# GpSimd's sums and splits on VectorE, and the first norm's modulation on ScalarE

## Chip, core and metric

One core of a Trainium2 chip runs the kernel once. The metric is the time of the execution on the device in microseconds (us). Five engines work on the core: TensorE (PE in the profile; its weight loads are PEld), VectorE (DVE), ScalarE (ACT), GpSimd (POOL) and SyncE (SP), which issues most of the DMAs. Each has a queue of its own and takes its instructions in order.

## What is computed

One layer of a decoder block in fp32: D = 1024 channels, S = 1024 tokens, a hidden width of 2816. The conditioning vector c gives nine vectors of shift, gain and gate by one product with ada_w. Three branches follow each other, and each begins with an RMS norm and a modulation:

```python
cs = jax.nn.silu(c)
mod = (cs @ ada_w[l] + ada_b[l]).reshape(B, N_MOD, D_MODEL)
sh1, sc1, g1, sh2, sc2, g2, sh3, sc3, g3 = [mod[:, j, None, :] for j in range(N_MOD)]
h = rms_norm(x, norm_ffn1[l]) * (1.0 + sc1) + sh1
x = x + FFN_RESIDUAL * g1 * swiglu(h, ffn1_w_in[l], ffn1_w_out[l])
h = rms_norm(x, norm_mix[l]) * (1.0 + sc2) + sh2
x = x + g2 * token_mixer(h, lb_all[l], mix_w_in[l], ...)
h = rms_norm(x, norm_ffn2[l]) * (1.0 + sc3) + sh3
x = x + FFN_RESIDUAL * g3 * swiglu(h, ffn2_w_in[l], ffn2_w_out[l])
return rms_norm(x, norm_final)
```

rms_norm(x, g) is x / sqrt(mean(x * x) + eps) * g over the channels of a token.

## The kernel before

x lies transposed in SBUF: a tile has 128 channels by 512 tokens. So x is 2 halves of the tokens (h = 0, 1) by 8 tiles of channels (k = 0 to 7), and a norm needs, for each half, a sum of squares over the 8 tiles and then over the partitions.

**Split products.** A product in fp32 is made of three matmuls in fp32r. `split` (L89) makes the two parts of an operand: ScalarE casts the high part (L90), and another engine subtracts it from the source for the low part (L91): VectorE, or GpSimd where `eng` says so. `mmw` (L229) then adds high x high (L232), high x low of the data (L233) and low of the weight x high (L234) in PSUM.

**The three openings.** `paired` (L242) computes the first projections of FFN1, of the token mixer ("mix") and of FFN2. It makes pairs of column blocks by a scheme with 7 products in place of 8, which needs sums of x tiles and of weight tiles. The first two column blocks (`fs`) are computed in the plain way while these sums are still missing; this is the opening: 192 matmuls (2 column blocks, 2 banks, 2 halves, 8 k, 3 parts). `warm_load` loads their weights and splits them, 8 splits of 128x512, the low parts on GpSimd (L268). Behind the opening GpSimd makes 16 subtractions of x tiles (L290), in place; their results are split into `t1` to `t4` by VectorE and ScalarE. `prepare` (L302) loads the weights of one pair of blocks and makes their four sums on VectorE (L306 and L251) and their splits. The loop over the other blocks begins with `prepare` of the first of them.

**The norm.** `squares` (L201) squares the tiles on ScalarE and adds them on VectorE, seven dependent additions (L211). `rows` (L182) sums over the partitions with small matmuls (L188), computes 1/rms of the 512 tokens in `rstd` (L174 to L179) and spreads it: four 128x128 instructions on VectorE (L196) and one matmul (L198) leave r, 128 x 512, in PSUM. `scaled` (L214) multiplies a tile by its column of the gain and by r in one VectorE instruction (L215) and adds the column of the shift on ScalarE (L216).

**FFN1's opening** (`warm` in `run`, L703) has the vectors of its own modulation to compute: for each k two accumulations of 128x1024 on VectorE (`mod`, L154, tiles `ada`), an addition of the bias to each (`mod_bias`, L159), and for the gain one instruction more (`mod_gain`, L163). Then, for each half, `scaled`, the split of the tile (`h` or `bq`), and the matmuls.

A scheduler orders the instructions of each queue by priorities, which follow from the order in which the program is written, and by free buffers: raw weights (tag `raw`) have 3 buffers, split weights (`w`) 11, the parts in `hq` 8 and in `bq` 4.

Of the kernel before, what the change touches and what calls it, by code (L numbers as in the profile page):

```python
# [11 lines left out]
AF = mybir.ActivationFunctionType  # L12
ALU = mybir.AluOpType
# [4 lines left out]
D = 1024  # L18
S = 1024
T = 512  # L20
NK = 8
# [12 lines left out]
C_N1, C_NM, C_N2, C_NF, C_LB, C_HG, C_CB, C_LG, C_LBI = 0, 8, 16, 24, 32, 48, 56, 64, 72  # L34
C_AB = 80
# [5 lines left out]
class Block:  # L41
# [200 lines left out]
    def paired(self, ctx, h, hctx, src, order, warm, emit, after, right, ready=()):  # L242


        nc = self.nc
        V, A = nc.vector, nc.scalar
        sub, add = ALU.subtract, ALU.add
        fs = order[:2]

        def tt(dst, a, b):  # L250
            V.tensor_tensor(dst, a, b, op=sub)  # L251

        def load(f):
            rs = []
            for b in range(2):
                rs.append(self.rp.tile([P, D], F32, tag="raw", name=self.nm("ra")))
                nc.sync.dma_start(rs[b], src(f, b))
            return rs

        self.part(ctx, wp=11, hq=8, bq=4)  # L260
        wop = lambda x: self.parts(x, self.wp, "w")
        hq = lambda x: self.parts(x, self.hq, "hq")


        ws, banks, b1 = {}, {}, dict(ready)

        def warm_load(f):
            ws[f] = [[self.parts(r[:, i * T:(i + 1) * T], self.wp, "w", nc.gpsimd) for i in range(2)] for r in load(f)]  # L268

        def warm_parts(hh, k):  # L270
            if (hh, k) not in b1:
                b1[hh, k] = self.parts(h[1][k], self.bq, "bq") if hh == 1 and k < 4 else self.parts(h[hh][k])

        def warm_mm(f, hh, k):
            if k == 0:
                banks[f, hh] = [self.acc() if f == fs[0] else self.bank() for _ in range(2)]
            for b in range(2):
                self.mmw(banks[f, hh][b], ws[f][b][k // 4], k % 4, b1[hh, k], k == 0, k == NK - 1)

        def warm_end(hh):  # L280
            for f in fs:
                emit(f, hh, *banks[f, hh], None)

        warm(fs, warm_load, warm_parts, warm_mm, warm_end)
        b11, b21, b22 = ([b1[hh, k0 + i] for i in range(4)] for hh, k0 in ((0, 0), (0, 4), (1, 4)))
        t1, t2, t3, t4 = [], [], [], []
        for i in range(4):
            x11, x12, x21, x22 = h[0][i], h[1][i], h[0][4 + i], h[1][4 + i]
            for o, x, y in ((x11, x12, x11), (x12, x22, x12), (x22, x22, x11), (x21, x21, x22)):
                nc.gpsimd.tensor_tensor(o, x, y, op=sub)  # L290
            t2.append(hq(x22))
            t3.append(hq(x12))
            t1.append(self.parts(x11))
            t4.append(self.parts(x21, self.bq, "bq"))
        hctx.close()
        self.part(ctx, right=True, **right)

        def product(ps, w, xs):
            for i in range(4):
                self.mmw(ps, w, i, xs[i], i == 0, i == 3)  # L300

        def prepare(f):  # L302
            ra, rb = load(f)
            a11, a12, a21, a22 = ra[:, :T], ra[:, T:], rb[:, :T], rb[:, T:]
            w11, w12, w22 = wop(a11), wop(a12), wop(a22)
            V.tensor_tensor(a22, a21, a22, op=add)  # L306
            tt(a21, a11, a21)
            tt(a11, a22, a11)
            tt(a12, a12, a11)
            ws2, ws3, ws1, ws4 = wop(a11), wop(a21), wop(a22), wop(a12)  # L310
            return w11, w12, w22, ws1, ws2, ws3, ws4

        ops = None
        for n, f in enumerate(order):
            if f not in fs:
                w11, w12, w22, ws1, ws2, ws3, ws4 = ops if ops else prepare(f)
                ops = prepare(order[n + 1]) if n + 1 < len(order) else None
                p1, p2, p3, p4, p5, p6, p7 = [self.acc() if (7 * n + i) % 2 == 0 else self.bank() for i in range(7)]
                product(p1, w11, b11)
                c11, c21, c22, u = (self.piece() for _ in range(4))  # L320
                A.copy(u, p1)
                product(p2, w12, b21)
                V.tensor_tensor(c11, p2, u, op=add)
                product(p3, ws2, t2)
                V.tensor_tensor(u, p3, u, op=add)
                product(p4, ws3, t3)
                V.tensor_tensor(c22, p4, u, op=add)
                product(p5, w22, t4)
                V.tensor_tensor(c21, p5, c22, op=add)
                emit(f, 0, c11, c21, c21)  # L330
                product(p6, ws1, t1)
                V.tensor_tensor(c22, p6, c22, op=add)
                V.tensor_tensor(u, p6, u, op=add)
                product(p7, ws4, b22)
                V.tensor_tensor(u, p7, u, op=add)  # L335
                emit(f, 1, u, c22, c22)
            after(n, f)
        return b1
# [338 lines left out]
    def run(self):  # L677
        nc, tc, a = self.nc, self.tc, self.a
# [16 lines left out]
        with outer:  # L695
# [7 lines left out]
            def warm(fs, load, parts, mm, end):  # L703
                ada = {}

                def mod_in(k):
                    ada[k] = [self.mod_load(j, k, p, t) for j, p, t in ((1, self.hp, "h"), (0, self.hq, "hq"))]

                def x_in(h):
                    for i in range(4):  # L710
                        nc.sync.dma_start(xt[h][i], a["x"][h, i])

                x_in(0)
                load(fs[0])
                mod_in(0)
                x_in(1)
                mod_in(1)
                mod_in(2)
                r = [self.rows(self.squares(xs[h]), D) for h in range(2)]
                for k in range(NK):  # L720
                    if k + 3 < NK:
                        mod_in(k + 3)
                    if k == 1:
                        load(fs[1])
                    for j in (1, 0):
                        self.mod(j, k, ada[k][1 - j])
                        self.mod_bias(j, k, k + 1)
                    self.mod_gain(1, C_N1, k, k + 1)
                    for h in range(2):
                        self.scaled(xs[h][k], k, r[h], m[1], m[0])  # L730
                        parts(h, k)
                        mm(fs[0], h, k)
                        if k == 2:
                            mm(fs[1], h, 0)
                            mm(fs[1], h, 1)
                        if k >= 2:
                            mm(fs[1], h, k)
                for h in range(2):
                    end(h)
# [282 lines left out]
```

## Time and profile before

| | before |
|---|---|
| median of 3 runs | 2467.28 us (2462.15 to 2468.1) |
| the profiled execution | 2467.12 us |
| its span, first to last instruction | 2465.3 us |
| TensorE busy | 2405.5 us, 98% |
| VectorE busy | 2010.2 us, 82% |
| ScalarE busy | 944.8 us, 38% |
| GpSimd busy | 116.9 us, 5% |

Busy time counts how long an engine had an instruction in work; matmuls overlap in their pipeline, so that one shows 0.39 us where the next starts 0.23 us later. The granted clock (PEclk) is the share of full speed that TensorE was given: 1.00 is 2.4 GHz, and its other level is 1.2 GHz. A time in brackets at the end of a row is the engine's idle time ahead of it, with what ended it.

### The profile page before, as it was taken

How to read it: one execution, taken by the hardware profiler on the slowest of the kernel's cores; microseconds unless marked ns; L12 is line 12 of the kernel's file. 1: busy time of each engine (PE TensorE's matmuls, PEld its weight loads, DVE VectorE, ACT ScalarE, POOL GpSimd, SP SyncE). 2: the span in 40 equal slices, each digit the busy share in tenths (PEclk: the TensorE clock that was granted, in tenths of full speed). 3: DMA queues.
4: the chain of work that ended last, by engine and by line, in shares of the span. 5: the costliest groups of instructions: out<-in, count | busy, mean ns of one | idle time of the engine just before them, and what ended most of it. 6: DMA issues, size and time to landing. Idle time of an engine off the chain costs nothing.

```text
span 2465.3 us, 30875 instructions
## 1 busy us (share of the span) xinstructions
PE 2405.5 (98%) x11320; PEld 1992.7 (81%) x11320; DVE 2010.2 (82%) x3010; ACT 944.8 (38%) x1679; POOL 116.9 (5%) x77
## 2 busy tenths in 40 slices
PE   4999999999999999999999999999999999999997
PEld 3788887888878888788888888888888888888886
DVE  8999999778889999799999877575568777775977
ACT  4522223344644333233333335453343333324443
POOL 3300000000050000000000000000050000000000
PEclk9999999999999999999999999999999999999998
DMA  7156665595523323311212112774523233228743
GB/s 277 68 190 208 202 203 186 174 344 176 171 86 116 106 83 104 105 52 65 68 44 65 56 56 90 241 251 162 159 80 124 86 107 117 93 86 298 269 128 124
DMA packets 139975, 346.46 MB, mean 141 GB/s; under 512 B 15536, under 2 KB 15664, under 8 KB 139824
## 3 DMA queue, kind: packets, MB, share of 16 engines
q1 hardware_dynamic: 139680, 343.97, 41.7%
q8 instruction: 89, 1.46, 0.2%
q10 hardware_dynamic: 144, 0.52, 0.1%
q14 instruction: 62, 0.51, 0.1%
HBM read 266.31 MB, written 78.12 MB: 140 GB/s over the span
## 4 chain that ended last, share of the span: by engine, by line
PE 80%; DVE 12%; DMA 5%; issue 2%; ACT 1%; POOL 0%; SPq 0%; DVEq 0%; ACTq 0%
PE pa L233 8%; PE pa L234 8%; PE pa L232 8%; PE pb L232 8%; PE pb L234 8%; PE pb L233 8%; PE pa L106 8%; PE pa L104 8%; PE pa L105 8%; PE pb L579 3%; DMA ada<-in_ada_w_dram 2%; DVE w L91 2%; DMA ra<-in_ffn_w_in_dram 1%; DVE ada L154 1%; DVE ra L251 1%
## 5 line engine op out<-in xcount | busy, mean ns | idle before, releaser
L90 ACT CAST w<-ra 128x512 fp32r<-128x512 f32 x402 | 238.4, 619 | 436.5 <-DMA ra<-in_ffn_w_in_dram 110.8
L104 PE MATMUL pa<-h,wh 128*128 128x512 f32 x896 | 355.4, 397 | 1.5 <-ACT wh L90 1.5
L106 PE MATMUL pa<-h,wl 128*128 128x512 f32 x896 | 353.7, 395 | 1.8 <-DVE wl L91 1.8
L105 PE MATMUL pa<-h,wh 128*128 128x512 f32 x896 | 353.3, 394 | 0.0
L543 DVE SCALAR_TENSOR_TENSOR uc<-u,par,uc 128x1023 f32<-128x1023 f32 (+14 forms) x240 | 303.1, 1263 | 2.7
L91 DVE TENSOR_TENSOR w<-ra,w 128x512 fp32r<-128x512 f32 x378 | 254.8, 690 | 10.0 <-ACT w L90 9.4
L232 PE MATMUL pa<-h,w 128*128 128x512 f32 x504 | 199.3, 398 | 5.8 <-ACT h L90 4.1
L233 PE MATMUL pa<-h,w 128*128 128x512 f32 x504 | 199.7, 396 | 2.9 <-DVE h L91 2.9
L234 PE MATMUL pb<-h,w 128*128 128x512 f32 x504 | 197.4, 392 | 4.1 <-POOL w L91 4.0
L234 PE MATMUL pa<-h,w 128*128 128x512 f32 x504 | 198.1, 393 | 0.0
L106 PEld LDWEIGHTS pa<-h,wl 128*128 128x128 f32 x896 | 168.6, 188 | 36.0 <-DVE wl L91 2.5
L104 PEld LDWEIGHTS pa<-h,wh 128*128 128x128 f32 x896 | 168.8, 188 | 35.3 <-ACT wh L90 2.3
L233 PE MATMUL pb<-h,w 128*128 128x512 f32 x504 | 197.0, 391 | 0.0
L232 PE MATMUL pb<-h,w 128*128 128x512 f32 x504 | 196.7, 391 | 0.0
L105 PEld LDWEIGHTS pa<-h,wh 128*128 128x128 f32 x896 | 168.9, 189 | 33.2 <-issue 0.7
L90 ACT CAST ob<-br 128x512 fp32r<-128x512 f32 x154 | 95.8, 622 | 198.6 <-PE pb L234 80.1
L90 ACT CAST wh<-raw 128x1024 fp32r<-128x1024 f32 x80 | 84.0, 1051 | 205.5 <-PE pa L105 192.6
L91 DVE TENSOR_TENSOR ob<-br,ob 128x512 fp32r<-128x512 f32 x154 | 106.7, 694 | 67.5 <-ACT ob L90 66.8
L233 PE MATMUL pa<-ob,oa 128*128 128x512 f32 x352 | 137.5, 391 | 1.5 <-DVE ob L91 1.5
L232 PE MATMUL pa<-ob,oa 128*128 128x512 f32 x352 | 137.1, 390 | 0.0
L234 PE MATMUL pa<-ob,oa 128*128 128x512 f32 x352 | 137.0, 389 | 0.0
L360 ACT ACTIVATE s<-c 128x512 f32<-128x512 f32 x80 | 50.6, 633 | 185.4 <-DVE c L335 127.6
(233 smaller groups left out, 5015.6 us busy)
## 6 DMA issues: line engine op xcount, KB each, us to landing
ra<-in_ffn_w_in_dram SPq DMA_DIRECT2D x88, 512.0 KB, 4.2
br<-bd SPq DMA_DIRECT2D x154, 256.0 KB, 3.2
bd<-c SPq DMA_DIRECT2D x146, 256.0 KB, 2.0
ada<-in_ada_w_dram SPq DMA_DIRECT2D x72, 512.0 KB, 4.4
ar<-in_ffn_w_out_dram SPq DMA_DIRECT2D x88, 256.0 KB, 4.5
ra<-in_mix_w_in_dram SPq DMA_DIRECT2D x32, 512.0 KB, 3.8
raw<-in_mix_w_in_dram SPq DMA_DIRECT2D x32, 512.0 KB, 3.5
ar<-in_ffn_w_out_dram SPq DMA_DIRECT2D x22, 512.0 KB, 4.8
```

What stands on the lines that cost most here:

```text
L90: self.nc.scalar.copy(hi, src)
L91: (eng or self.nc.vector).tensor_tensor(lo, src, hi.bitcast(F32), op=ALU.subtract)
L104: mm(ps, wh, x[:, 0, :], start=first, stop=False)
L105: mm(ps, wh, x[:, 1, :], start=False, stop=False)
L106: mm(ps, wl, x[:, 0, :], start=False, stop=last)
L154: self.nc.vector.scalar_tensor_tensor(raw, raw, 1.0, self.cs, op0=ALU.mult, op1=ALU.mult, accum_out=dst)
L232: mm(ps, wh, x[:, 0, :], start=first, stop=False)
L233: mm(ps, wh, x[:, 1, :], start=False, stop=False)
L234: mm(ps, wl, x[:, 0, :], start=False, stop=last)
L360: A.activation(s, a, AF.Silu)
L543: V.scalar_tensor_tensor(uc[:, j:], u[:, :S - j], cw(KC - 1 - j), uc[:, j:], op0=ALU.mult, op1=ALU.add)
L579: mm(ps[0:n, i * 64:(i + 1) * 64], ch(k, i)[:, 0:n], two(ch(qa, i))[:, :, 1, :], start=True, stop=True)
```

## The change

Three edits, in `paired` and in FFN1's opening.

- In `warm_load` the low parts of the first weights are made by VectorE, not GpSimd: 8 splits in each of the three openings.
- The 16 subtractions of x tiles go from GpSimd to VectorE, in the order of four loops and not of one, and `prepare` of the first pair of blocks is written ahead of them. GpSimd is left with a few memsets.
- In FFN1's opening each tile of a half is multiplied by r as soon as r of this half is there (L733 in the new file), all eight tiles ahead of the loop over k. In the loop ScalarE computes the gain and the shift of 128x1 from the accumulations (L742, L743), and applies both to a tile in one instruction (L746). The bias of the gain is prepared once for all k (L728). `mod_bias`, `mod_gain` and `scaled` are no longer used here.

```diff
         def warm_load(f):
-            ws[f] = [[self.parts(r[:, i * T:(i + 1) * T], self.wp, "w", nc.gpsimd) for i in range(2)] for r in load(f)]
+            ws[f] = [[self.parts(r[:, i * T:(i + 1) * T], self.wp, "w") for i in range(2)] for r in load(f)]
...
-        t1, t2, t3, t4 = [], [], [], []
-        for i in range(4):
-            x11, x12, x21, x22 = h[0][i], h[1][i], h[0][4 + i], h[1][4 + i]
-            for o, x, y in ((x11, x12, x11), (x12, x22, x12), (x22, x22, x11), (x21, x21, x22)):
-                nc.gpsimd.tensor_tensor(o, x, y, op=sub)
-            t2.append(hq(x22))
-            t3.append(hq(x12))
-            t1.append(self.parts(x11))
-            t4.append(self.parts(x21, self.bq, "bq"))
-        hctx.close()
...
-        ops = None
+        ops = prepare(order[2])
+
+
+        t1, t2, t3, t4 = [], [], [], []
+        xx = [(h[0][i], h[1][i], h[0][4 + i], h[1][4 + i]) for i in range(4)]
+        for x11, x12, x21, x22 in xx:
+            tt(x11, x12, x11)
+        for x11, x12, x21, x22 in xx:
+            tt(x12, x22, x12)
+            tt(x22, x22, x11)
+            t2.append(hq(x22))
+            t3.append(hq(x12))
+        for x11, x12, x21, x22 in xx:
+            tt(x21, x21, x22)
+            t4.append(self.parts(x21, self.bq, "bq"))
+        for x11, x12, x21, x22 in xx:
+            t1.append(self.parts(x11))
+        hctx.close()
...
-                w11, w12, w22, ws1, ws2, ws3, ws4 = ops if ops else prepare(f)
+                w11, w12, w22, ws1, ws2, ws3, ws4 = ops
...
-                r = [self.rows(self.squares(xs[h]), D) for h in range(2)]
+
+                bg = self.small(NK)
+                V.scalar_tensor_tensor(bg, self.par[:, C_AB + NK:C_AB + 2 * NK], 1.0, self.par[:, C_N1:C_N1 + NK],
+                                       op0=ALU.add, op1=ALU.mult)
+                for h in range(2):
+                    r = self.rows(self.squares(xs[h]), D)
+                    for x in xs[h]:
+                        V.tensor_tensor(x, x, r, op=ALU.mult)
...
+                    gain, shift = m[1][:, k:k + 1], m[0][:, k:k + 1]
                     for j in (1, 0):
                         self.mod(j, k, ada[k][1 - j])
-                        self.mod_bias(j, k, k + 1)
-                    self.mod_gain(1, C_N1, k, k + 1)
+                    A.activation(gain, gain, AF.Identity, bias=bg[:, k:k + 1], scale=self.col(C_N1, k))
+                    A.activation(shift, shift, AF.Identity, bias=self.col(C_AB, k))
                     for h in range(2):
-                        self.scaled(xs[h][k], k, r[h], m[1], m[0])
+                        x = xs[h][k]
+                        A.activation(x, x, AF.Identity, bias=shift, scale=gain)
```

How the queue of VectorE changes is shown at three places. The first is FFN1's opening, from the spread of r of half 1 on (`pb_450` before, `pb_460` now). Tiles `x_311` to `x_314` hold half 0 (two k each), `x_315` to `x_318` half 1; `h_514` and `bq_476` are parts of k = 1 of half 0 and of k = 0 of half 1. Before:

```order
L196 TENSOR_SCALAR s_445<-par,t_437 128x128 x4
L159 TENSOR_TENSOR mod_88<-mod_88,par 128x1
L154 SCALAR_TENSOR_TENSOR ada_362,mod_87<-ada_362,cs 128x1024
L215 SCALAR_TENSOR_TENSOR x_315<-x_315,mod_88,pb_450 128x512
L91 TENSOR_TENSOR h_514<-x_311,h_514 128x512
L215 SCALAR_TENSOR_TENSOR x_315<-x_315,mod_88,pb_450 128x512
L159 TENSOR_TENSOR mod_87<-mod_87,par 128x1
L163 SCALAR_TENSOR_TENSOR mod_88<-mod_88,par 128x1
L91 TENSOR_TENSOR bq_476<-x_315,bq_476 128x512
```

Now, where `w_510` to `w_519` are splits of the second column block's weights and `bq_491` is the part of k = 0 of half 1:

```order
L154 SCALAR_TENSOR_TENSOR ada_470,mod_87<-ada_470,cs 128x1024
L179 SCALAR_TENSOR_TENSOR t_447<-t_448,t_447 128x4
L91 TENSOR_TENSOR w_510<-ra_506,w_510 128x512
L196 TENSOR_SCALAR s_455<-par,t_447 128x128 x4
L91 TENSOR_TENSOR w_513<-ra_506,w_513 128x512
L91 TENSOR_TENSOR w_516<-ra_508,w_516 128x512
L733 TENSOR_TENSOR x_315<-x_315,pb_460 128x512 x2
L733 TENSOR_TENSOR x_316<-x_316,pb_460 128x512 x2
L733 TENSOR_TENSOR x_317<-x_317,pb_460 128x512 x2
L733 TENSOR_TENSOR x_318<-x_318,pb_460 128x512 x2
L91 TENSOR_TENSOR bq_491<-x_315,bq_491 128x512
```

All eight multiplications of the half and three weight splits now stand ahead of its first split. The second place is the mix opening, ahead of the last additions for r of its half 1 (L211). L444 is L451 in the new file (the residual of FFN1); `w_6380` and `w_6300` begin the weights of the first pair. Before:

```order
L444 SCALAR_TENSOR_TENSOR x_4014<-pa_5677,mod_89,x_4014 128x512
L211 TENSOR_TENSOR s_5994<-s_5994,s_6005 128x512
L444 SCALAR_TENSOR_TENSOR x_4014<-pa_5678,mod_89,x_4014 128x512
L444 SCALAR_TENSOR_TENSOR x_4015<-pa_5679,mod_89,x_4015 128x512
L211 TENSOR_TENSOR s_5994<-s_5994,s_6008 128x512
L91 TENSOR_TENSOR w_6380<-ra_6376,w_6380 128x512
L211 TENSOR_TENSOR s_5994<-s_5994,s_6011 128x512
L444 SCALAR_TENSOR_TENSOR x_4015<-pa_5680,mod_89,x_4015 128x512
L91 TENSOR_TENSOR w_6383<-ra_6376,w_6383 128x512
L91 TENSOR_TENSOR w_6386<-ra_6378,w_6386 128x512
L211 TENSOR_TENSOR s_5994<-s_5994,s_6014 128x512
```

Now, from the third L451 on (two more pairs of such splits, `w_5956` to `w_5965`, stand between the first three):

```order
L451 SCALAR_TENSOR_TENSOR x_4009<-pa_5673,mod_89,x_4009 128x512
L91 TENSOR_TENSOR w_5978<-ra_5970,w_5978 128x512
L91 TENSOR_TENSOR w_5981<-ra_5970,w_5981 128x512
L451 SCALAR_TENSOR_TENSOR x_4009<-pa_5674,mod_89,x_4009 128x512
L211 TENSOR_TENSOR s_5988<-s_5988,s_5999 128x512
L91 TENSOR_TENSOR w_6300<-ra_6296,w_6300 128x512
L211 TENSOR_TENSOR s_5988<-s_5988,s_6002 128x512
L91 TENSOR_TENSOR w_6303<-ra_6296,w_6303 128x512
L211 TENSOR_TENSOR s_5988<-s_5988,s_6005 128x512
L91 TENSOR_TENSOR w_6306<-ra_6298,w_6306 128x512
L211 TENSOR_TENSOR s_5988<-s_5988,s_6008 128x512
```

The eight weight splits have come between the four L451, and the last four additions stand behind all of these. The third place is FFN2's opening, around the last addition for r of its half 1. L948 is L964 in the new file (the residual of the token mixer). Before:

```order
L948 SCALAR_TENSOR_TENSOR x_12730<-pa_14367,mod_92,x_12730 128x512
L211 TENSOR_TENSOR s_14500<-s_14500,s_14517 128x512
L948 SCALAR_TENSOR_TENSOR x_12730<-pa_14399,mod_92,x_12730 128x512
L211 TENSOR_TENSOR s_14500<-s_14500,s_14520 128x512
L174 TENSOR_SCALAR t_14528<-pb_14523 128x4
```

Now:

```order
L964 SCALAR_TENSOR_TENSOR x_12724<-pa_14361,mod_92,x_12724 128x512
L91 TENSOR_TENSOR w_14442<-ra_14438,w_14442 128x512
L91 TENSOR_TENSOR w_14445<-ra_14438,w_14445 128x512
L91 TENSOR_TENSOR w_14448<-ra_14440,w_14448 128x512
L91 TENSOR_TENSOR w_14451<-ra_14440,w_14451 128x512
L91 TENSOR_TENSOR w_14458<-ra_14454,w_14458 128x512
L91 TENSOR_TENSOR w_14461<-ra_14454,w_14461 128x512
L211 TENSOR_TENSOR s_14494<-s_14494,s_14514 128x512
L174 TENSOR_SCALAR t_14522<-pb_14517 128x4
```

Six weight splits have come between the last residual and the last addition.

## Rows read from the trace of the kernel before

**Rows 1.** The page: busy time, share of the span and instructions of each engine.

```profile
PE 2405.5 (98%) x11320; PEld 1992.7 (81%) x11320; DVE 2010.2 (82%) x3010; ACT 944.8 (38%) x1679; POOL 116.9 (5%) x77
```

**Rows 2.** Busy time by stretch: length, PE, PEld, DVE, ACT, POOL, granted clock, DMA.

```profile
32.00:98.00 66.00, 55.75 (x194) 40.72 (x195) 65.04 (x104) 34.03 (x58) 35.43 (x20) 0.92 0.20 75
98.00:680.00 582.00, 579.65 (x2548) 476.71 (x2547) 503.50 (x833) 216.46 (x381) 0.00 (x0) 1.00 0.61 204
680.00:720.00 40.00, 36.01 (x146) 28.88 (x145) 29.00 (x48) 19.21 (x33) 15.21 (x11) 0.91 0.30 98
720.00:1000.00 280.00, 280.00 (x1237) 231.91 (x1237) 259.63 (x340) 102.61 (x176) 23.87 (x15) 1.00 0.29 99
1800.00:1860.00 60.00, 60.00 (x268) 49.32 (x267) 46.72 (x60) 31.44 (x57) 36.23 (x24) 1.00 0.19 66
```

**Rows 3.** Waits of TensorE, 32 to 98 us: total, times, longest.

```profile
PE pa L232 <- ACT h L90: 4.1, 3, 2.4
PE pb L234 <- POOL w L91: 4.0, 1, 4.0
PE pa L233 <- DVE h L91: 2.9, 5, 0.9
```

**Rows 4.** Timeline of GpSimd in FFN1's opening: start, length, instruction.

```profile
44.55 3.67 POOL L91 TENSOR_TENSOR w<-ra,w 128x512 fp32r<-128x512 f32 x2 [1.52 <-ACT w L90]
```

**Rows 5.** GpSimd's groups by line: busy, mean ns, idle before.

```profile
L290 POOL TENSOR_TENSOR x<-x,x 128x512 f32<-128x512 f32 x48 | 79.8, 1683 | 55.2 <-ACT x L216 37.9 <-issue 6.6 <-DVE h L91 3.9
L91 POOL TENSOR_TENSOR w<-ra,w 128x512 fp32r<-128x512 f32 x24 | 36.1, 1533 | 1423.6 <-ACT w L90 1423.6
```

**Rows 6.** Timeline of VectorE in FFN1's opening.

```profile
34.15 1.22 DVE L154 SCALAR_TENSOR_TENSOR ada<-ada,cs 128x1024 f32<-128x1024 f32 x1
...
38.34 0.75 DVE L215 SCALAR_TENSOR_TENSOR x<-x,mod,pb 128x512 f32<-128x512 f32 x1 [0.96 <-PE pb L198]
...
41.21 0.68 DVE L91 TENSOR_TENSOR bq<-x,bq 128x512 fp32r<-128x512 f32 x1
...
45.31 1.77 DVE L91 TENSOR_TENSOR h<-x,h 128x512 fp32r<-128x512 f32 x1
47.00 1.24 DVE L159 TENSOR_TENSOR mod<-mod,par 128x1 f32<-128x1 f32 x1
...
56.92 0.68 DVE L91 TENSOR_TENSOR h<-x,h 128x512 fp32r<-128x512 f32 x1
```

**Rows 7.** Timeline of TensorE in FFN1's opening and at its end.

```profile
52.82 0.79 PE L234 MATMUL pb<-h,w 128*128 128x512 f32 x1 [4.02 <-POOL w L91]
...
70.59 0.73 PE L232 MATMUL pa<-h,w 128*128 128x512 f32 x2 [2.40 <-ACT h L90]
...
98.01 0.39 PE L232 MATMUL pa<-h,w 128*128 128x512 f32 x1
```

**Rows 8.** Timeline of ScalarE, a shift of the first norm.

```profile
26.26 0.72 ACT L216 ACTIVATE x<-x,mod 128x512 f32<-128x512 f32 x1 [3.71 <-DVE x L215]
```

**Rows 9.** Timeline of TensorE at the mix opening.

```profile
689.83 0.50 PE L233 MATMUL pa<-ob,oa 128*128 128x512 f32 x1 [1.05 <-DVE ob L91]
...
703.05 1.87 PE L188 MATMUL pb<-ones,s 128*128 128x1 f32 x8 [2.95 <-DVE s L211]
```

**Rows 10.** Timeline of VectorE ahead of the mix opening and in it.

```profile
673.07 4.29 DVE L91 TENSOR_TENSOR h<-x,h 128x512 fp32r<-128x512 f32 x7
...
711.82 5.36 DVE L215 SCALAR_TENSOR_TENSOR x<-x,mod,pb 128x512 f32<-128x512 f32 x8 [3.48 <-PE pb L198]
...
720.74 5.87 DVE L91 TENSOR_TENSOR bq<-x,bq 128x512 fp32r<-128x512 f32 x4 [1.04 <-ACT bq L90]
```

**Rows 11.** Timeline of VectorE in FFN2's opening.

```profile
1811.66 0.69 DVE L211 TENSOR_TENSOR s<-s,s 128x512 f32<-128x512 f32 x1 [0.76 <-ACT s L210]
...
1818.13 5.36 DVE L215 SCALAR_TENSOR_TENSOR x<-x,mod,pb 128x512 f32<-128x512 f32 x8 [1.22 <-PE pb L198]
...
1827.69 4.69 DVE L91 TENSOR_TENSOR bq<-x,bq 128x512 fp32r<-128x512 f32 x4
```

More of the change, by code (lines that the diff above doesn't have):

```diff
@@ L285, in paired @@
         b11, b21, b22 = ([b1[hh, k0 + i] for i in range(4)] for hh, k0 in ((0, 0), (0, 4), (1, 4)))
-        t1, t2, t3, t4 = [], [], [], []
-        for i in range(4):
-            x11, x12, x21, x22 = h[0][i], h[1][i], h[0][4 + i], h[1][4 + i]
-            for o, x, y in ((x11, x12, x11), (x12, x22, x12), (x22, x22, x11), (x21, x21, x22)):
-                nc.gpsimd.tensor_tensor(o, x, y, op=sub)
-            t2.append(hq(x22))
-            t3.append(hq(x12))
-            t1.append(self.parts(x11))
-            t4.append(self.parts(x21, self.bq, "bq"))
-        hctx.close()
[L296 to L300, printed above, removed]
         def prepare(f):
@@ L311, in prepare, with product @@
             return w11, w12, w22, ws1, ws2, ws3, ws4
-        ops = None
+        ops = prepare(order[2])
[14 more added lines that the diff above has]
+        hctx.close()
+        self.part(ctx, right=True, **right)
+        def product(ps, w, xs):
+            for i in range(4):
+                self.mmw(ps, w, i, xs[i], i == 0, i == 3)
         for n, f in enumerate(order):
             if f not in fs:
-                w11, w12, w22, ws1, ws2, ws3, ws4 = ops if ops else prepare(f)
+                w11, w12, w22, ws1, ws2, ws3, ws4 = ops
                 ops = prepare(order[n + 1]) if n + 1 < len(order) else None
```

## The prediction

> **What bounds the kernel now.** I read the busy times first. TensorE is busy 2405.5 of 2465.3 us [rows 1], so only its idle time and its slow stretches can be won back. The table by stretches shows where they are: from 98 to 680 us TensorE is busy 579.65 of 582.00 us, and from 720 to 1000 us all of the time; what the change can reach of the rest lies in 32 to 98 us and, a little, in 680 to 720 us [rows 2]. GpSimd works in just these places: 35.43 us in 32 to 98, 15.21 in 680 to 720, 36.23 in 1800 to 1860, where TensorE is full nevertheless [rows 2].
>
> In 32 to 98 us TensorE runs 194 matmuls [rows 2]. At the steady pitch, 280.00 / 1237 = 0.226 us each [rows 2], they need 43.9 us; 22.1 us are lost. Named waits are 4.1 us for ScalarE's and 2.9 for VectorE's halves of the data, and one of 4.0 us for a weight split on GpSimd [rows 3]; the rest is the lower level of the clock: the granted clock of the stretch is 0.92 [rows 2], a mixture of 1.2 and 2.4 GHz. VectorE is busy 65.04 of the 66.00 us [rows 2]: the data pieces come late because VectorE is full. So VectorE is the bound of this opening, and the steady stretch begins at 98.01 us, at the first of the seven products [rows 7].
>
> VectorE is full partly because its own instructions are long there. A split takes 0.68 us at 56.92, and 1.77 us at 45.31 [rows 6], while two splits of GpSimd's run from 44.55 to 48.22 [rows 4]; a 128x1 addition took 1.24 us at 47.00 [rows 6]. The lines with an operand in PSUM are spared: L215 takes 0.75 us at 38.34 [rows 6] and 0.67 each at 711.82 [rows 10], and no more where it falls inside a piece of GpSimd's.
>
> **The change, part by part.** All sums are made against the profiled execution, 2467.12 us, of which the span is 2465.3; the median of the three is 2467.28, so the one stands for the other.
>
> *GpSimd's work on VectorE.* Each of the three openings (FFN1, mix, FFN2) gives up 8 splits (1.53 us each on GpSimd) and 16 subtractions (1.68 each) [rows 5]. On VectorE an undisturbed 128x512 split or subtraction fills 0.61 us (4.29 for seven in a row) [rows 10]: 24 x 0.61 = 14.6 us more per opening. Against it goes the lengthening. In 32 to 98 us I count about 10 us on splits (up to 1.1 each) and 7 us on the tiny additions, some 17 in all, of which the pairs in rows 6 are samples; the bound from above is all of GpSimd's 35.43 us [rows 2], from below nothing. So VectorE's total hardly moves; what moves is when TensorE is served.
>
> *The first norm.* The 24 small instructions L159 and L163 go; their cost is in the 7 us above. L215 becomes L733 at the same price, 0.67 us with the PSUM operand [rows 10]. ScalarE gets two 128x1 instructions per k and its 16 modulations take a second column operand; no row shows that form, the nearest is L216 with one, 0.72 us [rows 8]. ScalarE is busy 34.03 of 66.00 us [rows 2], so neither is on the path, apart from one in the chain of the first piece. The Trainium skill ("ScalarE: Activation LUTs", What ACT_TABLE_LOAD costs) states about 93 ns for each pointer operand of 128x1, which no run here shows: by it the estimate is 1.5 us on ScalarE, and the sum would be at most 0.3 us higher.
>
> More weighs the order. Of each half all eight multiplications now stand together ahead of its first piece, and all wait for r of that half. I walk VectorE's queue: the first r comes at about 24.6 (it was read at 25.5: four weight splits of 0.6 are put in front of the last addition, the tiny instructions out of it). Four additions are finished by then or shortly after, at 25.5; eight multiplications to 30.9; first piece split at 32.1. The last addition of half 1 ends at 34.5, its row sums are ready 2.2 later at 36.7 (1.87 us of L188 at the lower clock [rows 9] and its way), and five ada accumulations (1.15 us pitch, a row of 1.22) [rows 6], two splits and the tiny instructions stand between there and the spread, which ends at 42.7. The broadcast waits 1.22 us at 1818.13 [rows 11] at full clock; I take 2.2 at the lower one, which gives r of half 1 at 44.9, against 38.34 before [rows 6]. Eight multiplications, 5.3 us, and a split: the first piece of half 1 is whole at 50.8, against 41.9 [rows 6]. Queued behind these multiplications are three weight splits and the splits of all further pieces, and TensorE waits for them.
>
> From there on VectorE needs, per k, two ada accumulations and two splits, 2.3 + 1.2 = 3.5 us; TensorE needs 24 x 0.226 = 5.4. TensorE becomes the bound. By the order 32 of the 192 opening matmuls stand ahead of that piece, 160 behind it: 160 x 0.226 = 36.2 us, so the opening ends at 87.0 at full clock; I add 1 us for a start at the lower level, as behind the waits at 52.82 and 70.59 [rows 7]: 88. The 16 sums, 4 weight sums and the splits that feed the products then stand on VectorE from about 71 to 96; by the same walk the third piece of the second sums is whole at 91 and wanted at 95.5. So **FFN1: 88 against 98, -10 us**, from -12 (no slow stretch, r 1 us earlier) to -6 (two more waits with the slow stretch behind them, 2 us each). The stretch up to 680 is full, so it passes on the whole gain.
>
> *Mix opening.* Before, a split lengthened under GpSimd made TensorE wait 1.05 us at 689.83, and the row sums L188 came 2.95 us late, at 703.05, and took 1.87 us [rows 9], since the clock had gone to its lower level (0.91 in the mean of the stretch [rows 2]). Now VectorE has the eight weight splits between the four L451, which it can hold (1.2 us in a spacing of 2.0), then four additions and three splits, 7 x 0.6 to 0.7, ending near 700.9; 24 matmuls stand ahead of L188 where 15 did, 5.4 us from about 695.3, so TensorE reaches it at 700.8. The wait is nearly gone and with it the slow stretch: 1.2 + 2.9 + about 2: **-6 us**, from -7.5 to -3 (the last addition waits for the third split's data). VectorE's 16 sums lie later, where TensorE was busy 280.00 of 280.00 us beside a VectorE at 259.63 [rows 2], and four splits there take 5.87 us at 720.74 [rows 10] where 2.4 would do.
>
> *FFN2 opening.* Here GpSimd was beside a full TensorE [rows 2], so there is nothing to win. VectorE now has six weight splits between the last L964 (0.75 us from about 1810.2) and the last addition, which began at 1811.66 [rows 11]: the first split is whole at 1811.5, and the third matmul, wanted at 1810.4, waits 1.1 us; the last addition ends at 1815.1, when TensorE has come to L188 as well. Four more splits stand around the spread, so L215 starts at about 1820.7 against 1818.13; the pieces of half 1, split from 1827.69 on [rows 11], still come before TensorE has finished half 0 at about 1835. **+1.4 us**, from 0 to +4 (a slow stretch behind the wait).
>
> Sum: -10 - 6 + 1.4 = -14.6; 2467.12 - 14.6 = 2452.5 us. The ends together are -19.5 and -5; not all fall to one side, so the forecast's own range is 2447 to 2459.
>
> **Rivals.**
> 1. *Half of FFN1's gain goes again.* r of half 1 comes 6.6 us later; if TensorE idles around it more than I give it, stays at the lower level through the first matmuls and stops once more at the weights of the second column, FFN1 gains 4 to 5 us. For it: the two starts in rows 7 each cost more than the wait itself. Against: behind 50.8 VectorE is ahead. Time: 2467.1 - 4.5 - 6 + 1.4 = 2458, 2456 to 2462.
> 2. *VectorE stays the bound.* In its queue four evaluations of the opening's results (L368), which wait for TensorE and ScalarE, stand ahead of the second half of the sums. If they hold the sums up by more than the 4.5 us of margin, the products start 4 us late, and FFN2 shows its +4: 2467.1 - 6 - 6 + 4 = 2459, 2456 to 2463.
> 3. *Slower.* The lengthening isn't GpSimd's doing but comes from DMA or from VectorE itself, and stays. Then 14.6 us per opening are added to a VectorE that is full at 65.04 of 66.00: FFN1 +12, mix +4, FFN2 +2 gives 2485. It decides against me if L91 in 40 to 80 us still has 1.7 us. Against it: the lengthened one at 45.31 lies inside GpSimd's own splits, the short one at 56.92 does not [rows 4, 6], and the PSUM form was spared. The Trainium skill ("SBUF — State Buffer", SBUF: two separate sides) says that a VectorE instruction with two SBUF inputs and a GpSimd instruction that reads SBUF lock each other out for the whole instruction; the trace agrees with the direction, at 1.77 against 0.68 us.
>
> **How the numbers follow.** The forecast has 0.64, rival 1 0.18, rival 2 0.12, rival 3 0.06. What a measurement can tell from no change is about 0.3%, 7.4 us: faster is below 2459.9, slower above 2474.7. The forecast lies wholly below; of rivals 1 and 2 some two fifths lie above. Faster 0.82, same 0.12, slower 0.06. The range leaves out rival 3 and the ends of the others: 2446 to 2461.
>
> **What would show it.** Right: L91 and the small additions in 32 to 98 us at 0.6 to 0.7 us throughout; first piece of half 1 near 51 us and no named wait of TensorE above 1 us behind it; first product at 86 to 90; L188 of the mix opening at 0.95 us without a wait; about 1 us of wait at the third matmul of FFN2. Wrong: a granted clock under 0.95 in 60 to 88 us (rival 1), TensorE waiting for sums behind 88 (rival 2), or splits of 1.7 us without GpSimd (rival 3).

## The result: 21 us faster, outside the range

The changed kernel takes 2444.38 us (median of 4 runs, 2443.83 to 2445.03) against 2465.51 before (2462.15 to 2468.1): a ratio of 0.9915, 95% interval 0.9898 to 0.9932. The direction was forecast, the size was not: 2452.5 was predicted, with 2446 to 2461 as the range.

The page of the changed kernel has GpSimd idle and VectorE no fuller than before, as [rows 1] has it for the kernel before:

```profile
PE 2395.2 (98%) x11320; PEld 1987.2 (81%) x11320; DVE 2000.2 (82%) x3059; ACT 953.2 (39%) x1695; POOL 1.2 (0%) x5
```

The stretches of [rows 2], in the changed kernel (length, PE, PEld, DVE, ACT, POOL, granted clock, DMA):

```profile
32.00:98.00 66.00, 63.01 (x254) 49.42 (x253) 64.00 (x115) 43.81 (x81) 0.00 (x0) 1.00 0.28 103
98.00:680.00 582.00, 581.78 (x2566) 480.43 (x2565) 508.42 (x844) 221.94 (x389) 0.00 (x0) 1.00 0.60 203
680.00:720.00 40.00, 39.40 (x176) 32.00 (x175) 37.27 (x68) 25.22 (x45) 0.00 (x0) 1.00 0.33 119
```

In 32 to 98 us TensorE runs 254 matmuls where 194 ran. The granted clock in that row, 1.00 (0.92 before), says nothing of the row's first 12 us: in both kernels a matmul there still takes 0.63 us, as it does before behind the wait at 52.82 [rows 7], and 0.39 us only from about 45 us on. In the changed kernel:

```profile
40.34 0.63 PE L234 MATMUL pa<-h,w 128*128 128x512 f32 x1
...
45.14 0.39 PE L233 MATMUL pb<-h,w 128*128 128x512 f32 x1
```

From there on the changed kernel stays at full clock, where the kernel before fell back twice (0.54 granted from 54 to 58 us, 0.66 from 70 to 74). In 98 to 680 us, a stretch that I had called full, it runs 18 matmuls more.

Where the time went is read best from a few marks that both programs pass in TensorE's timeline: the first matmul of FFN1's third product (its operand is the first `hq`), the first matmul of the mix opening, the third product of mix, the first matmul of FFN2, the last L188. "Before again" is a second profile of the unchanged kernel, run e5 below.

| stretch, us | before | before again | changed | change (against each profile) | forecast |
|---|---|---|---|---|---|
| start to FFN1's third product | 103.45 | 104.05 | 91.27 | -12.2, -12.8 | -10 |
| to the mix opening | 593.09 | 590.72 | 587.85 | -5.2, -2.9 | -1.2 (put down to the mix opening) |
| to mix's third product | 57.06 | 56.68 | 51.66 | -5.4, -5.0 | -4.8 |
| to FFN2's first matmul | 1056.35 | 1056.19 | 1056.29 | -0.1, +0.1 | 0 |
| to the last L188 | 640.69 | 641.13 | 642.30 | +1.6, +1.2 | +1.4 |
| to the end | 14.66 | 13.93 | 13.83 | -0.8, -0.1 | 0 |
| span | 2465.3 | 2462.7 | 2443.2 | -22.1, -19.5 | -14.6 |

A second profile of the changed kernel (e10) has 91.22, 586.88, 51.40, 1059.14, 642.05 and 14.53 us in these stretches. One of them is 2.9 us longer than in the first profile of the same kernel. So a difference of this size in a single pair of profiles proves little; below, a stretch counts where several profiles agree.

In FFN1's opening TensorE's waits were 11.0 us in [rows 3]; in the changed kernel, 32 to 98 us, all of them lie ahead of 49 us:

```profile
PE pa L233 <- DVE h L91: 2.9, 2, 2.7
PE pa L232 <- ACT h L90: 1.8, 1, 1.8
PE pb L232 <- DVE x L733: 0.6, 1, 0.6
PE pb L188 <- DVE s L211: 0.3, 1, 0.3
```

VectorE's instructions are short, as the groups by line of the changed kernel say (busy, mean ns, idle before):

```profile
L91 DVE TENSOR_TENSOR h<-x,h 128x512 fp32r<-128x512 f32 x48 | 30.6, 684 | 0.0
...
L91 DVE TENSOR_TENSOR hq<-x,hq 128x512 fp32r<-128x512 f32 x24 | 15.4, 686 | 0.0
```

The same two groups of the kernel before:

```profile
L91 DVE TENSOR_TENSOR h<-x,h 128x512 fp32r<-128x512 f32 x48 | 48.1, 1034 | 0.0
...
L91 DVE TENSOR_TENSOR hq<-x,hq 128x512 fp32r<-128x512 f32 x24 | 26.9, 1157 | 0.0
```

That is 29 us less for these 72 splits alone; it pays most of the 44 us that the 72 instructions taken over from GpSimd cost on VectorE, at 0.61 us each.

### The profile page after: what moved, and what is told of

The parts are those of the page before. It is cut to its first block, busy times and chain, and to the rows that moved or that the text cites. A ratio compares the mean times of both kernels' runs of the same rounds, so it can differ in the third digit from the quotient of the medians.

```text
span 2443.2 us, 30741 instructions
## 1 busy us (share of the span) xinstructions
PE 2395.2 (98%) x11320; PEld 1987.2 (81%) x11320; DVE 2000.2 (82%) x3059; ACT 953.2 (39%) x1695; POOL 1.2 (0%) x5
## 4 chain that ended last, share of the span: by engine, by line
PE 95%; DVE 3%; DMA 1%; ACT 1%; issue 0%; SPq 0%; DVEq 0%; ACTq 0%
PE pa L233 11%; PE pa L234 11%; PE pa L232 11%; PE pb L234 10%; PE pb L233 10%; PE pb L232 10%; PE pa L106 8%; PE pa L105 8%; PE pa L104 8%; PE pb L586 4%; PE pb L610 1%; PE pb L625 1%; PE pb L645 1%; PE pb L570 1%; PE pb L647 1%; DVE s L211 0%
## 5 line engine op out<-in xcount | busy, mean ns | idle before, releaser
L91 DVE TENSOR_TENSOR w<-ra,w 128x512 fp32r<-128x512 f32 x402 | 266.7, 687 | 14.5 <-ACT w L90 13.7
```

The lines of the kernel that those rows point to most:

```text
L91: (eng or self.nc.vector).tensor_tensor(lo, src, hi.bitcast(F32), op=ALU.subtract)
```

## The experiments

Each run was compared with the kernel before on the same chip; medians of before were 2464.4 to 2465.7. The three edits of the change were first made one by one.

### e1: the new norm alone

```diff
-                r = [self.rows(self.squares(xs[h]), D) for h in range(2)]
+                for h in range(2):
+                    r = self.rows(self.squares(xs[h]), D)
+                    for x in xs[h]:
+                        V.tensor_tensor(x, x, r, op=ALU.mult)
...
-                        self.scaled(xs[h][k], k, r[h], m[1], m[0])
+                        A.activation(x, x, AF.Identity, bias=shift, scale=gain)
```

> The kernel before with the new first norm alone; GpSimd keeps its splits and sums. Theory A (GpSimd's lengthening of VectorE is what makes FFN1's opening long): splits of up to 1.7 us stay, the first of the seven products still begins at about 96 us against 98.0, total 2464 to 2467 against 2466. Rival B (the gain of the opening is the norm's: fewer small instructions in VectorE's queue): first product near 88 us, total about 2456.

It took 2468.81 us, ratio 1.0019 (1.0010 to 1.0028): 4 us slower than before, and neither theory's time. Its trace shows both a gain and a larger loss. TensorE, 60 to 100 us, in two stretches:

```profile
60.00:80.00 20.00, 20.00 (x90) 16.57 (x89) 20.00 (x21) 13.77 (x27) 13.69 (x8) 1.00 0.00 0
80.00:100.00 20.00, 10.29 (x45) 7.93 (x43) 19.86 (x25) 6.39 (x12) 6.72 (x5) 0.82 0.00 0
```

From 47.6 us on the opening's matmuls run without a gap beside a working GpSimd, and they are done at 90.1 us, 8 us sooner than before. Then TensorE stops, and the first product begins at 101.78:

```profile
101.78 0.80 PE L232 MATMUL pa<-h,w 128*128 128x512 f32 x1 [11.49 <-ACT s L360]
```

ScalarE's timeline there names the chain:

```profile
88.81 0.62 ACT L90 CAST bq<-x 128x512 fp32r<-128x512 f32 x1
98.16 1.66 ACT L90 CAST w<-ra 128x512 fp32r<-128x512 f32 x3 [8.73 <-DVE ra L251]
99.84 1.28 ACT L360 ACT_TABLE_LOAD   x1
101.13 0.60 ACT L360 ACTIVATE s<-pa 128x512 f32<-128x512 f32 x1
```

The product needs the PSUM bank of an opening result. Its evaluation (L360) stands in ScalarE's queue behind the casts of the first pair's weights, which wait 8.73 us for their sums (L251) on VectorE. There splits still take up to 1.78 us beside GpSimd (1.06 us in the mean of all 48 splits of `h`). So the opening can end early without GpSimd's release; what follows it cannot begin.

### e2: GpSimd's work on VectorE alone

```diff
-            ws[f] = [[self.parts(r[:, i * T:(i + 1) * T], self.wp, "w", nc.gpsimd) for i in range(2)] for r in load(f)]
+            ws[f] = [[self.parts(r[:, i * T:(i + 1) * T], self.wp, "w") for i in range(2)] for r in load(f)]
...
-                nc.gpsimd.tensor_tensor(o, x, y, op=sub)
+                tt(o, x, y)
```

> The kernel before with the splits and sums on VectorE, in the old order of the sums, weights of the first pair prepared behind them, old norm. Theory A: first product at about 88 us, mix opening 5 to 6 us shorter, FFN2's about 2 us longer, the stall of 4 us between 340 and 400 us stays, total about 2454. Rival B: first product at 94 or later, total about 2460. Rival C (the stall at 340 to 400 us goes because VectorE is less loaded): no stall, about 2450.

2453.12 us, ratio 0.9955 (0.9940 to 0.9970), near theory A's 2454. But the parts differ: the opening is done at 86.5 us, sooner than A said, and the products behind it wait, as TensorE's timeline shows:

```profile
91.57 0.50 PE L234 MATMUL pa<-h,w 128*128 128x512 f32 x1 [3.98 <-DVE w L91]
...
100.05 0.49 PE L232 MATMUL pa<-hq,w 128*128 128x512 f32 x1 [2.03 <-ACT w L90]
```

A split of the first pair's weights comes too late. And the stretch to the mix opening is 587.1 us, without the loss of before, as rival C had it.

### e3 and e4: the early preparation, added to before and taken from the changed kernel

e3 is the kernel before with this edit alone (the function `prepare` moves up with its call); e4 is the changed kernel with the edit undone.

```diff
+        ops = prepare(order[2])
         t1, t2, t3, t4 = [], [], [], []
...
-        ops = None
...
-                w11, w12, w22, ws1, ws2, ws3, ws4 = ops if ops else prepare(f)
+                w11, w12, w22, ws1, ws2, ws3, ws4 = ops
```

> The kernel before with one edit: the weights of the first pair are prepared ahead of the sums, as in the changed kernel; GpSimd and norm as before. Theory D (the stall of 4 us between 340 and 400 us is the weight loads running out of lead, and the early preparation gives the lead): stall gone, total about 2462. Rival E (the stall is chance in the one profiled execution of before): total within 1 us of before's median, and other executions of before without it.

> The changed kernel with one edit: the weights of the first pair are prepared behind the sums, when the loop over the pairs begins. Theory D: the lead is lost, TensorE waits 4 us or more between 86 and 400 us, total about 2449 against 2444.4. Rival E: no stall, total 2444 to 2445.

e3 took 2462.2 us, ratio 0.9988 (0.9978 to 0.9998); e4 2449.76, ratio 0.9942 (0.9927 to 0.9957). e4's total is what theory D said, but not for D's reason. Its stretch to the mix opening is 587.3 us, with no stall; the whole 6.7 us lie at the start of the products, 97.95 against 91.27, in one wait and in the slow matmuls of 0.63 us that follow it up to 96.2:

```profile
90.49 0.79 PE L234 MATMUL pa<-h,w 128*128 128x512 f32 x1 [3.70 <-DVE w L91]
```

So the early preparation doesn't buy lead for later; it buys the first product's weights. In e3, where TensorE comes to the products only at 99.6, they would have been there anyway, and the total falls by 2 us, of which the stretch behind (588.8 us) has more than all. That is theory D's total, but e1 (588.3) and e2 (587.1) lack the stall too, and they prepare late.

### e5: the kernel before once more

> The kernel before once more, unchanged, for a second profile of it. From the first of the seven products' third (first hq operand) to the start of the mix opening the first profile of before took 593.1 us, and the four kernels run since took 587.1 to 588.8. Rival E (chance of one execution): this profile takes 587 to 589 there and its total is about 2461 to 2463. Theory D': the stall belongs to the order of before and shows again at 592 to 594 us.

2464.46 us, with 590.7 us to the mix opening: between the two ranges. The stall is there again, at the same place and with the same name; TensorE in the second profile:

```profile
389.10 0.50 PE L232 MATMUL pa<-h,w 128*128 128x512 f32 x1 [1.34 <-ACT c L321]
```

and the copy that it waits for, in ScalarE's timeline of the first profile:

```profile
387.95 1.66 ACT L90 CAST w<-ra 128x512 fp32r<-128x512 f32 x3 [1.97 <-DVE ra L251]
389.52 0.58 ACT L321 COPY c<-pa 128x512 f32<-128x512 f32 x1
```

The copy of the first product out of PSUM stands behind three casts that wait for weight sums. So the place belongs to the kernel, and the size varies from one execution to the next: the stretch is 2.9 to 5.2 us longer than in the changed kernel, of which the wait of 1.05 us at its end [rows 9] is a part.

### e6 and e12: sums, or splits, back on GpSimd

Both are the changed kernel with one part of the move undone.

```diff
+        gg = lambda dst, a, b: nc.gpsimd.tensor_tensor(dst, a, b, op=sub)
...
-            tt(x11, x12, x11)
+            gg(x11, x12, x11)
...
-            ws[f] = [[self.parts(r[:, i * T:(i + 1) * T], self.wp, "w") for i in range(2)] for r in load(f)]
+            ws[f] = [[self.parts(r[:, i * T:(i + 1) * T], self.wp, "w", nc.gpsimd) for i in range(2)] for r in load(f)]
```

The last two lines are e12, the others e6, where each of the 16 `tt` of x tiles becomes a `gg`.

> The changed kernel with the 48 subtractions of x tiles back on GpSimd, in the new order; splits stay on VectorE. If it is the sums that must come off GpSimd: the first product still starts at 86 us, but the third, which needs the sums, waits for them, since GpSimd needs 16 x 1.68 = 27 us from about 70; 4 to 8 us lost in FFN1, splits of VectorE lengthened to 1.7 us behind 70 us, total 2449 to 2453. If the splits alone carried the gain: 2444 to 2446.

> The changed kernel with only the 24 opening weight splits back on GpSimd; sums stay on VectorE. By the walk of the prediction FFN1 loses little (the eight splits lie at 14 to 17 and 40 to 43 us, ahead of the point where TensorE becomes the bound), the mix opening waits again by 1 to 3 us for lengthened additions, FFN2 gains 1.5: 2443 to 2447. If a lengthened VectorE at the opening's start holds up the pieces: TensorE waits inside FFN1's opening, 2448 to 2453.

e6 took 2456.46 us, ratio 0.9964 (0.9951 to 0.9977): all of its 12 us lie ahead of the third product (103.17). That is above both ranges: I had the first product at 86 us and the third waiting for its sums. In fact the opening itself is held up by a wait of 2.27 us, and the first product, at 95.62, waits 5.60 us for ScalarE's L368. As in e1 this stands behind casts that come late, here one that waits 5.20 us for GpSimd's subtractions. Mix and FFN2 don't mind: 51.5 and 641.9 us.

e12 took 2453.65, ratio 0.9960 (0.9945 to 0.9975), 9 us more than the changed kernel, near the second of my ranges and not the first. The mix opening gives back 5.3 us: L188 waits 2.94 us again, as in [rows 9]. So its gain is the splits' and nothing else. FFN1 gives back 3.9, by an instruction that I had not thought of. GpSimd's and VectorE's timelines of e12:

```profile
42.40 5.18 POOL L91 TENSOR_TENSOR w<-ra,w 128x512 fp32r<-128x512 f32 x4 [22.95 <-DMA ra<-in_ffn_w_in_dram]
```

```profile
42.69 4.97 DVE L196 TENSOR_SCALAR s<-par,t 128x128 f32<-128x128 f32 x4
49.87 4.86 DVE L733 TENSOR_TENSOR x<-x,pb 128x512 f32<-128x512 f32 x8
```

The spread of r, four instructions that take 0.86 us alone, takes 4.97 while GpSimd splits, and r of half 1 is read at 49.87 and not at 43.91. In e1 the same four take 4.99 us.

### e11: new norm and all moves, old order of the sums, late preparation

Against e4, the loops over the sums:

```diff
+        for i in range(4):
+            x11, x12, x21, x22 = h[0][i], h[1][i], h[0][4 + i], h[1][4 + i]
+            for o, x, y in ((x11, x12, x11), (x12, x22, x12), (x22, x22, x11), (x21, x21, x22)):
+                tt(o, x, y)
...
-        for x11, x12, x21, x22 in xx:
-            tt(x11, x12, x11)
-        for x11, x12, x21, x22 in xx:
-            tt(x12, x22, x12)
-            tt(x22, x22, x11)
...
-            tt(x21, x21, x22)
```

> The kernel before with the new norm and all of GpSimd's work on VectorE, but the old order of the sums and the weights of the first pair prepared behind them. The changed kernel with only that preparation late took 2449.8. If the order of the sums is worth nothing: 2449 to 2451. If it matters, because the second sums are wanted first: 2452 to 2455, with waits of TensorE for hq or w behind 86 us.

2450.61 us, ratio 0.9944 (0.9929 to 0.9958), against 2449.76 for e4: the new order of the sums by itself is worth nothing that these runs can tell.

### e7, e8, e9 and e10: what could still be had

e7 gives FFN2's eight opening splits back to GpSimd. e8 multiplies by r inside the loop over k, one tile of each half at a time. e9 does both. e10 is the changed kernel again, beside e9. In the cut below the lines up to `self.last = True`, which stands ahead of FFN2, are e7, the rest e8.

```diff
+        self.last = False
...
-            ws[f] = [[self.parts(r[:, i * T:(i + 1) * T], self.wp, "w") for i in range(2)] for r in load(f)]
+            ws[f] = [[self.parts(r[:, i * T:(i + 1) * T], self.wp, "w", nc.gpsimd if self.last else None) for i in range(2)] for r in load(f)]
...
+        self.last = True
...
-                for h in range(2):
-                    r = self.rows(self.squares(xs[h]), D)
-                    for x in xs[h]:
-                        V.tensor_tensor(x, x, r, op=ALU.mult)
+                r = [self.rows(self.squares(xs[h]), D) for h in range(2)]
...
                         x = xs[h][k]
+                        V.tensor_tensor(x, x, r[h], op=ALU.mult)
                         A.activation(x, x, AF.Identity, bias=shift, scale=gain)
```

> The changed kernel with only FFN2's eight opening splits back on GpSimd. By the profile of the changed kernel the third matmul of that opening waits 0.99 us for a split on VectorE, and the stretch from FFN2's start to the last row sums is 1.6 us longer than before. If the place of these splits is the cause: that wait is gone and the total is 1 to 2 us lower, 2442.5 to 2443.5. If the cause is elsewhere: 2444 to 2445, no difference.

> The changed kernel with the multiplication by r written inside the loop over k, one tile of each half at a time, ahead of ScalarE's modulation. If the block of eight multiplications of half 1 holds up TensorE: the first piece of half 1 comes up to 4 us sooner than 49.4, the opening ends at 82 to 84 us instead of 85.8, total 2441 to 2443. If VectorE then becomes the bound again (ada sums ahead of the multiplications): waits inside the opening, total 2444 to 2450.

> The changed kernel with both edits that each gave 1.5 us: the multiplication by r inside the loop over k, and FFN2's eight opening splits on GpSimd. They lie 1700 us apart, so they should add: 2440 to 2442, and no wait for a split in FFN2's opening. If one was chance: 2442 to 2443.5.

> The changed kernel once more, on the chip of the other runs of this set: 2443.5 to 2445.5, and the stretch from the third product to the mix opening 587 to 588.5 us again.

e7 took 2442.84 us, ratio 0.9907 (0.9893 to 0.9922); e8 2442.68, 0.9909 (0.9892 to 0.9925); e9 2442.14, 0.9910 (0.9896 to 0.9925); e10 2443.59, 0.9914 (0.9898 to 0.9931). The intervals overlap, so no total here is told apart from the changed kernel's. The traces say more. In e7 FFN2 is back at 640.1 us. In e8 the opening ends at 83.6 and the third product starts at 89.03, 2.2 us sooner; that is the price of eight multiplications ahead of the first piece. e9 keeps e8's gain but not e7's: GpSimd's last two splits now fall on the spread of r in FFN2, which takes 2.93 us in place of 0.88, and TensorE waits 1.83 us for it. The same wait shows in other runs with GpSimd's splits in FFN2's opening, 1.84 us in e1 and 0.83 us in the second profile of before, but not in the first, in e3 or in e12. Whether a split on GpSimd costs nothing there depends on an accident of a microsecond.

## Why the prediction was too small

Most of what it said of places and mechanisms held. One step failed, FFN1's term was 2 us too small, and the early preparation was left without a price of its own.

**"The stretch up to 680 is full, so it passes on the whole gain."** This step failed. The row that I took for full has 579.65 of 582.00 us and 2548 matmuls [rows 2]; the changed kernel has 2566 in a window of the same 582 us, or 0.2268 us each. 18 missing matmuls are 4.1 us. I had made just this count for 32 to 98 us and not here. All 18 are missing around the stall at 390 us that e5 shows. From 345 to 395 us, in before, before again, e3 and the changed kernel:

```profile
345.00:395.00 50.00, 47.92 (x204) 37.55 (x203) 45.26 (x76) 14.67 (x26) 0.00 (x0) 1.00 0.60 204
345.00:395.00 50.00, 48.52 (x212) 39.09 (x211) 46.38 (x78) 14.67 (x26) 0.00 (x0) 1.00 0.62 212
345.00:395.00 50.00, 49.84 (x219) 40.64 (x218) 45.69 (x76) 14.53 (x26) 0.00 (x0) 1.00 0.63 210
345.00:395.00 50.00, 50.00 (x222) 41.39 (x221) 47.67 (x81) 15.25 (x27) 0.00 (x0) 1.00 0.54 189
```

By the marks, the stretch gave 2.9 to 5.2 us where the prediction had 1.2, so the step hid 2 to 4 us. ScalarE waited for weight loads in 98 to 680 us, in the kernel before:

```profile
ACT w L90 <- DMA ra<-in_ffn_w_in_dram: 107.7, 27, 8.6
```

and in the changed one:

```profile
ACT w L90 <- DMA ra<-in_ffn_w_in_dram: 33.8, 26, 8.1
```

Less waiting goes with the change, but it isn't the cause of the gain: e2 has 109.8 us of it and no stall. Every edited kernel lost less there than the two profiles of before, 586.9 to 589.0 us, and e1, e2 and e3 did so with one edit each; so no one of the three is needed for it. The wait and its place are shown; which part of the order of ScalarE's and VectorE's queues sets it stays open.

**FFN1's opening: -12.2 for -10.** The walk along VectorE's queue was right in its order and a little slow in its prices. The changed kernel's timeline of VectorE:

```profile
25.27 4.87 DVE L733 TENSOR_TENSOR x<-x,pb 128x512 f32<-128x512 f32 x8
...
43.91 4.87 DVE L733 TENSOR_TENSOR x<-x,pb 128x512 f32<-128x512 f32 x8 [1.19 <-PE pb L198]
48.70 0.69 DVE L91 TENSOR_TENSOR bq<-x,bq 128x512 fp32r<-128x512 f32 x1
```

r of half 1 came at 43.91 (forecast 44.9). Eight multiplications took 4.87 us, 0.61 each: I had priced L733 by L215 [rows 10], another operation, at 0.67. The first piece of half 1 was whole at 49.39 (50.8). The 1 us for a start at the lower clock wasn't needed: the matmuls of the second column block, which the order puts ahead of that piece, kept TensorE at work from 42 us, and it was at its upper level when the piece came. 160 matmuls later the opening was done:

```profile
85.83 0.39 PE L232 MATMUL pa<-h,w 128*128 128x512 f32 x1
...
91.27 0.39 PE L232 MATMUL pa<-hq,w 128*128 128x512 f32 x1
```

85.83 for 88, and two full products behind it without a wait.

**What the -12 is made of.** The prediction put it on GpSimd's lengthening of VectorE, some 10 us on splits and 7 on the tiny additions. The single edits take the two parts away by different ways. The moves take GpSimd off: they alone end the opening 11.5 us sooner (e2). The norm takes the tiny instructions out of VectorE's queue: it alone ends the opening 8 us sooner with GpSimd still at work (e1). Those instructions, in VectorE's groups of the kernel before, 32 to 98 us, and one of them alone:

```profile
L159 DVE TENSOR_TENSOR mod<-mod,par 128x1 f32<-128x1 f32 x13 | 6.1, 467 | 0.0
L163 DVE SCALAR_TENSOR_TENSOR mod<-mod,par 128x1 f32<-128x1 f32 x7 | 4.2, 601 | 0.0
...
57.52 0.15 DVE L159 TENSOR_TENSOR mod<-mod,par 128x1 f32<-128x1 f32 x1
```

20 of them fill 10.3 us, where 3 would do at 0.15 us each: the 7 us of the prediction. What e1's new order of the queue adds to its 8 us, no run separates. The two gains don't add: together they end it at 85.83, and the changed kernel has no wait behind 49 us, so that TensorE itself is the bound there, as the walk had it. And neither edit keeps its gain in the products: there e1 waits 11.5 us, e2 some 4 and 2. In totals the norm alone is worth +4.4 us, the moves -11.3, the early preparation -2.2, which makes -9; the three and the new order of the sums together are worth -21. The early preparation, whose four sums and splits the prediction counted on VectorE but gave no price, is worth 5 to 7 us once the opening is short (e4). The margin of 4.5 us that I gave was for the x sums, and for these TensorE doesn't wait; what would have come late without the early preparation is the first product's weights.

**Mix opening: right.** L188 waits 0.60 us in the changed kernel (2.95 before [rows 9]) and takes 1.05; -5.4 us, and 1 us more ahead of it. e12 shows that the splits carry it.

**FFN2: right in place and size.** TensorE and VectorE in the changed kernel, against [rows 11]:

```profile
1788.67 0.50 PE L234 MATMUL pa<-h,w 128*128 128x512 f32 x1 [0.99 <-DVE w L91]
```

```profile
1787.94 3.69 DVE L91 TENSOR_TENSOR w<-ra,w 128x512 fp32r<-128x512 f32 x6
1791.55 0.68 DVE L211 TENSOR_TENSOR s<-s,s 128x512 f32<-128x512 f32 x1
...
1798.01 5.36 DVE L215 SCALAR_TENSOR_TENSOR x<-x,mod,pb 128x512 f32<-128x512 f32 x8
```

The third matmul waits 0.99 us (forecast 1.1), and the stretch is 1.2 to 1.6 us longer (1.4). By e7 it is these splits. That there was nothing to win here held for the first profile of before alone: in the second and in e1 GpSimd's splits cost TensorE 0.83 and 1.84 us at the spread of r, which the changed kernel can't meet.

**The end.** 0.8 us less than in the first profile of before, 0.1 than in the second; no term stood for it, and the two profiles of the changed kernel differ as much (13.83 and 14.53).

**The rivals.** Rival 1 didn't come: from 45 to 98 us TensorE shows the upper level, with one wait of 0.56 us. Rival 2 named a true danger in a kernel that avoids it: in e1 and e6 the evaluations of the opening's results (L360, L368) do hold up the products by 11.5 and 5.6 us, though in ScalarE's queue and not in VectorE's. Rival 3 fell: a split takes 684 ns without GpSimd.

**The range.** Against the first profile of before the terms came to -12.2 in FFN1, -6.6 at the mix opening and +1.6 in FFN2, -17.2 together. Only FFN1 reached its end of the three. That would be 2449.9 us, inside the range; the 4.0 us of the stretch that I had called full, and 0.8 at the end, lead to the 2445.03 us of the changed kernel's profiled execution, below it. Part of the miss is the start: the sums began at an execution of 2467.12 us, and the median of before is 2465.51.

## To carry to other kernels

Call a stretch full only after dividing it by the pitch of one matmul; a row at 99.6% held 4 us. Edits that relieve the same bound don't add up, and an edit that is worth little alone can be what lets the others through: ask of each stage what the next one will wait for if it ends sooner. Price an operation by the same operation with the same kinds of operands.

## What the runs showed of the hardware

GpSimd lengthens more on VectorE than subtractions of two SBUF tensors. Four 128x128 multiplications by a column (L196), one tensor from SBUF, took 4.99 us in e1, 4.97 in e12 and 2.93 in e9 beside GpSimd's splits, and 0.86 to 0.88 alone. Eight multiplications with one operand in PSUM (L733) take 4.87 us without GpSimd and 4.86 in e1, from 49.77 us on, while GpSimd subtracts from 51.81 to 55.62. That is in line with the Trainium skill ("SBUF — State Buffer", SBUF: two separate sides), which has the shared ports locked for whole instructions, against VectorE instructions with two SBUF inputs and against those in a two-port mode. Which of the two L196 is, no run here shows.

An ACTIVATE with two column operands takes 0.81 us where L216 with one takes 0.72 [rows 8], in the changed kernel's group:

```profile
L746 ACT ACTIVATE x<-x,mod,mod 128x512 f32<-128x512 f32 x16 | 12.4, 810 | 3.3 <-DVE x L733 3.1
```

0.09 us for the second agrees with the 93 ns of the Trainium skill ("ScalarE: Activation LUTs", What ACT_TABLE_LOAD costs), and nothing waited for it.
